# Norms by one power operation on GpSimd: a two-layer convolution, HGRN2 and retention block on one core

## The chip, the core and the metric

The kernel runs on one core of a Trainium2 chip. The metric is the device time of one execution in microseconds (us). An engine is named as in the profile: PE (TensorE, matrix products), PEld (its loading of weights), DVE (VectorE), ACT (ScalarE), POOL (GpSimd), SP (SyncE, which issues the transfers).

## What is computed

A block of two layers on 256 tokens of width 2048, in float32. In each layer the input is projected into ten parts; three mixers work on them (a causal convolution of 31 taps over 512 channels, a gated linear recurrence of 6 heads, a retention of 6 heads); their outputs go through `w_out`, and a feed-forward network of width 8192 follows. Behind both residual sums stands a layer norm over the width. Each mixer has a norm of its own too. All of them need one over the square root of a variance or a mean square:

```python
def layer_norm(x, g, b):                       # over 2048, and over 512 in the convolution
    mu = jnp.mean(xf, axis=-1, keepdims=True)
    var = jnp.mean(jnp.square(xf - mu), axis=-1, keepdims=True)
    return (xf - mu) * lax.rsqrt(var + LN_EPS) * g + b

# recurrence: over each head's 128 columns, no mean is subtracted
o = o * lax.rsqrt(jnp.mean(jnp.square(o), axis=-1, keepdims=True) + LN_EPS)
# retention: over each head's 128 columns
o = ((o - mu) * lax.rsqrt(var + LN_EPS)).reshape(b, t, D_RET) * gn_g + gn_b

for l in range(DEPTH):
    proj = jnp.einsum('btd,de->bte', x, w_in[l])
    ...
    h = jnp.einsum('bte,ed->btd', mix, w_out[l])
    x = layer_norm(DEEPNORM_ALPHA * x + h, ln1_g[l], ln1_b[l])
    f = jnp.square(jax.nn.relu(jnp.einsum('btd,df->btf', x, w_ff1[l])))
    h = jnp.einsum('btf,fd->btd', f, w_ff2[l])
    x = layer_norm(DEEPNORM_ALPHA * x + h, ln2_g[l], ln2_b[l])
```

## The kernel before

**Products.** Weights (440 MB with everything else) stream in by transfers of 1 MB on SP's queue into three `raw` buffers. Each half of a transfer is a unit: ACT rounds it (the high part, L288), and DVE subtracts to get the low part (L291), into one of six `wp` buffers; PE then multiplies three times (high by high, high by low, low by high). In `xstat` (products at L313) two token tiles of 128 take turns over eight units of 512 columns; in `wstat` (L363, L365) the features stand on the partitions. For the last column group ahead of a layer norm (`tail=6`) the first token tile ends six units ahead of the second, and behind it (`head=6`) the first token tile of the next phase runs six units ahead, so that each tile's norm lies beside the other tile's products. In those phases the low parts of units 1 and 3 are left to POOL (`POOL_LO`, also L291).

**A layer norm** (`Norm`, two token tiles each, four of them in the run) goes, for one tile: the last residual sum (L942 or L944) and its statistics (L869) on DVE, mean and variance (L879) on DVE, one over the square root on POOL (L422 to L430), meanwhile on DVE three operations `(y - mean) * g` (L887), then three `y * rstd + b` (L893) on DVE, and for the fourth chunk one scaling on ACT (L897); each chunk is transposed by PE (L399) and split into high and low parts by ACT (L388) and DVE (L390), which are the operand of the next products. In the last norm of the run there are four L887 and four L893, and eight transfers of the result instead of transpositions.

**A mixer's norm**: two heads by two token tiles give four runs of 128 columns in one tile of PSUM. `norm_stats` (L541, L543) takes mean and variance on DVE. POOL makes four inverse square roots per partition (L670 or L759, then L407 to L414 and, in retention, L761 to L763), ACT scales (L679 in `hgrn`, L770 in `ret`, L823 in `conv`), PE transposes (L399). There are six such norms in `hgrn` and six in `ret` over the two layers, and four in `conv`, whose inverse square root has the same form as a layer norm's.

**The order of the work** is a plan made when the kernel is built. Every operation is given to a list scheduler (`Plan`) with a cost in us, what it reads and what it writes. `run` sends each operation out in the order of its simulated start; 0.22 us lie between operations of different engines that depend on each other and 0.13 between those of one engine. Each engine then executes its queue strictly in that order. A cost in the plan thus decides where an operation stands in the queues, and not how long it takes. Large products are PE's own stream (`main`); the operations of a layer norm have priority (`FIRST`, `NOW`); of what can start within 0.12 us the scheduler takes the most urgent. The costs: `dve(n, ptr)` = 0.00104 n + 0.069 + 0.06 ptr, a weight split on POOL 2.35, one small POOL operation `POOLC` = 0.26, the twelve of a layer norm's inverse square root 2.6.

Of the kernel before, what the change touches and what calls it, by code (L numbers as in the profile page):

```python
# [202 lines left out]
def block_kernel(ctx: ExitStack, tc: tile.TileContext, a: dict, out: bass.AP):  # L203
# [30 lines left out]
    POOLC = 0.26  # L234

# [168 lines left out]
    def rsqrt(var, s, c0, n):  # L404
        """1/sqrt of var + EPS, [P, n], by Newton's iteration, to float32; columns c0.. of s are its own."""
        v, y, t = (s[:, c0 + i * n:c0 + (i + 1) * n] for i in range(3))
        G.tensor_scalar(out=v, in0=var, scalar1=EPS, scalar2=None, op0=ALU.add)  # L407
        G.tensor_scalar(out=y.bitcast(I32), in0=v.bitcast(I32), scalar1=-0.5, scalar2=float(0x5F3759DF),
                        op0=ALU.mult, op1=ALU.add)
        for _ in range(3):  # L410
            G.tensor_tensor(out=t, in0=y, in1=y, op=ALU.mult)  # L411
# [2 lines left out]
            G.tensor_tensor(out=y, in0=t, in1=y, op=ALU.mult)  # L414
        return y

    def rsqrt1(s, mean, var):
        """Columns 37, 48 of s: 1/sqrt(var + EPS) and -mean/sqrt(var + EPS), [P, 1], by Newton's iteration.
        The iterate is y times -2, 4, -8 in turn; v / 4, v / 16 make up for it."""
        v, v4, v16, y, t = (s[:, 52 + i:53 + i] for i in range(5))  # L420
        ts = G.tensor_scalar
        ts(out=v, in0=var, scalar1=EPS, scalar2=None, op0=ALU.add)  # L422
        ts(out=y.bitcast(I32), in0=v.bitcast(I32), scalar1=-0.5, scalar2=float(0x5F3759DF), op0=ALU.mult, op1=ALU.add)
        ts(out=v4, in0=v, scalar1=0.25, scalar2=None, op0=ALU.mult)
        ts(out=v16, in0=v, scalar1=0.0625, scalar2=None, op0=ALU.mult)
        for w in (v, v4, v16):
            ts(out=t, in0=y, scalar1=y, scalar2=w, op0=ALU.mult, op1=ALU.mult)  # L427
            ts(out=y, in0=t, scalar1=-3.0, scalar2=y, op0=ALU.add, op1=ALU.mult)  # L428
        ts(out=s[:, 37:38], in0=y, scalar1=-0.125, scalar2=None, op0=ALU.mult)  # L429
        ts(out=s[:, 48:49], in0=mean, scalar1=y, scalar2=0.125, op0=ALU.mult, op1=ALU.mult)  # L430
# [104 lines left out]
    def norm_stats(po, n, w):  # L535
        """Mean and variance (columns 24.. of the tile) of each of n runs of w columns."""
        s = sm.buf()

        def fn():
            for i in range(n):  # L540
                V.bn_stats(out=s.t[:, 6 * i:6 * i + 6], in_=po.t[:, i * w:(i + 1) * w])  # L541
            for i in range(n):
                V.bn_aggr(out=s.t[:, 24 + 2 * i:26 + 2 * i], in_=s.t[:, 6 * i:6 * i + 6])  # L543
# [49 lines left out]
    def hgrn(l, p, pair, gate, vt, mixT):
# [71 lines left out]
        s = norm_stats(po, 4, P)  # L665

        def rs():
            mv = s.t[:, 24:32].rearrange("p (n two) -> p n two", two=2)
# [1 line left out]
            G.tensor_tensor(out=q, in0=mv[:, :, 0], in1=mv[:, :, 0], op=ALU.mult)  # L670
# [49 lines left out]
    def ret(l, p, pair, gate, vt, mixT):  # L720
# [461 lines left out]
```

## Time and profile before

| | |
|---|---|
| median of three runs | 2399.02 us (2397.52 to 2400.28) |
| profiled execution, span | 2401.9 us |
| PE busy | 2343.3 us (98%) |
| DVE busy | 1505.0 us (63%) |
| ACT busy | 1052.9 us (44%) |
| POOL busy | 162.6 us (7%), 359 operations |
| read from memory | 432.74 MB, 181 GB/s over the span |

The profile is one execution; its span, 2401.9 us, is the only time it has of its own. A line of an operation gives the source line, the engine, the operation, its output and input tiles with their shapes, and how often it ran; in a timeline the first two numbers are the start and the length, and the brackets tell how long the engine had stood idle and what ended that. In a table of windows stand the stretch, its length, and the busy time of each engine; `PEclk` is the clock granted to PE, 1.00 at full speed. In the list of waits stand the total, the number and the longest one.

### The profile page before, as it was taken

How to read it: one execution, taken by the hardware profiler on the slowest of the kernel's cores; microseconds unless marked ns; L12 is line 12 of the kernel's file. 1: busy time of each engine (PE TensorE's matmuls, PEld its weight loads, DVE VectorE, ACT ScalarE, POOL GpSimd, SP SyncE). 2: the span in 40 equal slices, each digit the busy share in tenths (PEclk: the TensorE clock that was granted, in tenths of full speed). 3: DMA queues.
4: the chain of work that ended last, by engine and by line, in shares of the span. 5: the costliest groups of instructions: out<-in, count | busy, mean ns of one | idle time of the engine just before them, and what ended most of it. 6: DMA issues, size and time to landing. Idle time of an engine off the chain costs nothing.

```text
span 2401.9 us, 29886 instructions
## 1 busy us (share of the span) xinstructions
PE 2343.3 (98%) x12067; PEld 1986.8 (83%) x12067; DVE 1505.0 (63%) x2010; ACT 1052.9 (44%) x1334; POOL 162.6 (7%) x359
## 2 busy tenths in 40 slices
PE   9999999999999999999999999998999999999997
PEld 7888888788888888888778888887888888888886
DVE  6987565665465565565569975656655655655655
ACT  6435444354344344344344454443543443443441
POOL 0012021200000000000100031112000000000001
PEclk9999999999999999999999999999999999999999
DMA  8544556455555555556454445554555555555562
GB/s 287 181 158 144 181 176 202 158 184 186 195 181 192 193 190 188 195 182 217 160 169 161 162 149 169 191 202 152 190 193 193 180 190 193 191 193 193 178 228 103
DMA packets 67706, 439.91 MB, mean 183 GB/s; under 512 B 7664, under 2 KB 7920, under 8 KB 16624
## 3 DMA queue, kind: packets, MB, share of 16 engines
q1 hardware_dynamic: 67568, 438.01, 53.5%
q8 instruction: 94, 1.54, 0.2%
q14 instruction: 44, 0.36, 0.0%
HBM read 432.74 MB, written 2.10 MB: 181 GB/s over the span
## 4 chain that ended last, share of the span: by engine, by line
PE 88%; POOL 6%; issue 3%; DVE 2%; DMA 0%; ACT 0%; SPq 0%; DVEq 0%; POOLq 0%
PE mm L313 41%; PE mm L363 29%; PE mm L365 15%; PE aux L617 1%; PE aux L399 1%; DVE x_nat L893 1%; POOL sm L413 1%; POOL sm L411 1%; POOL sm L427 1%; POOL sm L412 1%; POOL sm L428 0%; DMA raw<-in_wv 0%; POOL sm L414 0%; DVE sm L541 0%; POOL sm L407 0%
## 5 line engine op out<-in xcount | busy, mean ns | idle before, releaser
L291 DVE TENSOR_TENSOR wp<-raw,wp 128x1024 fp32r<-128x1024 f32 (+1 forms) x796 | 970.8, 1220 | 626.8 <-ACT wp L288 624.7
L288 ACT CAST wp<-raw 128x1024 fp32r<-128x1024 f32 (+1 forms) x802 | 842.3, 1051 | 824.7 <-PE mm L313 567.7
L363 PE MATMUL mm<-act,wp 128*128 128x512 f32 x3328 | 1184.4, 400 | 0.0
L313 PE MATMUL mm<-wp,act 128*128 128x512 f32 x4608 | 1068.6, 392 | 3.5 <-ACT wp L288 2.5
L313 PEld LDWEIGHTS mm<-wp,act 128*128 128x128 f32 x4608 | 867.7, 189 | 184.5 <-ACT wp L288 3.5
L365 PE MATMUL mm<-act,wp 128*128 128x256 f32 x3328 | 934.9, 281 | 0.0
L363 PEld LDWEIGHTS mm<-act,wp 128*128 128x128 f32 x3328 | 627.2, 188 | 152.3
L365 PEld LDWEIGHTS mm<-act,wp 128*128 128x128 f32 x3328 | 629.8, 189 | 0.5
L372 ACT COPY r<-mm 128x256 f32<-128x256 f32 x208 | 77.9, 374 | 368.2 <-PE mm L365 368.0
L375 DVE TENSOR_TENSOR r<-mm,r 128x256 f32<-128x256 f32 x184 | 78.1, 425 | 152.5 <-ACT r L372 152.1
L422 POOL TENSOR_SCALAR sm<-sm 128x1 f32<-128x1 f32 x12 | 5.8, 486 | 1598.3 <-DVE sm L879 1594.7
L800 DVE SCALAR_TENSOR_TENSOR r<-u_t,cst,r 128x256 f32<-128x256 f32 x240 | 102.0, 479 | 0.0
L388 ACT CAST act<-r 128x512 fp32r<-128x512 f32 x82 | 51.1, 623 | 17.2 <-DVE r L1053 16.2
L390 DVE TENSOR_TENSOR act<-r,act 128x512 fp32r<-128x512 f32 x82 | 56.0, 683 | 3.9 <-ACT act L388 3.9
L893 DVE SCALAR_TENSOR_TENSOR x_nat<-x_nat,sm,r 128x512 f32<-128x512 f32 x26 | 30.5, 1231 | 22.4 <-POOL sm L429 22.4
L617 PEld LDWEIGHTS aux<-pair 128*128 128x128 f32 x336 | 42.4, 191 | 2.6
L1053 DVE SCALAR_TENSOR_TENSOR r<-r 128x512 f32<-128x512 f32 x60 | 41.6, 693 | 2.1
L399 PE MATMUL aux<-cst,x_nat 128*128 128x128 f32 x96 | 17.6, 335 | 25.2 <-DVE x_nat L893 16.4
L617 PE MATMUL aux<-pair 128*128 128x64 f32 x336 | 42.0, 267 | 0.0
L944 DVE TENSOR_TENSOR x_nat<-x_nat,mm 128x512 f32<-128x512 f32 x48 | 30.9, 681 | 12.6 <-PE mm L313 12.6
L399 PEld LDWEIGHTS aux<-cst,x_nat 128*128 128x128 f32 x96 | 13.4, 170 | 29.9 <-DVE x_nat L893 19.4
L670 POOL TENSOR_TENSOR sm<-sm 128x4 f32<-128x4 f32 x6 | 4.7, 790 | 424.1 <-DVE sm L543 424.1
(123 smaller groups left out, 661.3 us busy)
## 6 DMA issues: line engine op xcount, KB each, us to landing
raw<-in_w SPq DMA_DIRECT2D x248, 1024.0 KB, 4.8
raw<-in_wp SPq DMA_DIRECT2D x88, 1024.0 KB, 4.8
raw<-in_wo SPq DMA_DIRECT2D x32, 1024.0 KB, 4.8
raw<-in_wv SPq DMA_DIRECT2D x20, 1024.0 KB, 4.8
raw<-in_w1x SPq DMA_DIRECT2D x8, 1024.0 KB, 4.9
raw<-in_wv SPq DMA_DIRECT2D x6, 512.0 KB, 5.8
pair<-pair SPq DMA_DIRECT2D x24, 128.0 KB, 2.3
x_nat<-in_x SPq DMA_DIRECT2D x1, 2048.0 KB, 9.4
```

Source lines behind the costliest of these rows:

```text
L288: S.copy(out=u.w.t[:, 0, sl], in_=raw.t[:, rs])
L291: (G if pool_lo else V).tensor_tensor(out=u.w.t[:, 1, sl], in0=raw.t[:, rs], in1=u.w.t[:, 0, sl].bitcast(F32), op=ALU.subtract)
L313: nc.tensor.matmul(ps.t, lhsT=xT[k // 4].t[:, xs, k % 4, t * P:(t + 1) * P], rhs=w[:, ws, kb, :], start=(k == 0 and n == 0), stop=(k == KB ...
L363: nc.tensor.matmul(pv, lhsT=w[:, 0, kb, :], rhs=xt[:, :, k % 4, :], start=(k == 0), stop=False)
L365: nc.tensor.matmul(pv[:, 0, :], lhsT=w[:, 1, kb, :], rhs=xt[:, 0, k % 4, :], start=False, stop=(k == KB - 1))
L372: S.copy(out=low.t, in_=ps.t[:, T:])
L375: V.tensor_tensor(out=dst[2]()[:, b * T:(b + 1) * T], in0=ps.t[:, 0:T], in1=low.t, op=ALU.add)
L390: op("DVE", dve(n), lambda: V.tensor_tensor(out=x.t[:, 1, blks, cols], in0=bl(src(), nb), in1=x.t[:, 0, blks, cols].bitcast(F32), op=ALU.s ...
L399: nc.tensor.transpose(out=pt.t[:, i * P:(i + 1) * P], in_=src()[:, i * P:(i + 1) * P], identity=ident)
L617: nc.tensor.matmul(ps.t[:, b * 64:(b + 1) * 64], lhsT=Kt()[:, b * P:(b + 1) * P], rhs=rhs, start=True, stop=True)
L800: V.scalar_tensor_tensor(out=d, in0=src, scalar=cw[:, l, b, j:j + 1], in1=d, op0=ALU.mult, op1=ALU.add)
L893: op("DVE", dve(W, 1), lambda c=c: V.scalar_tensor_tensor(out=self.y(t, c), in0=self.y(t, c), scalar=rstd(), in1=self.gb[c][1].t, op0=ALU. ...
```

## The change

Newton's iteration (an estimate by integer arithmetic on the bits, then three steps) is taken out. A constant tile `mhalf` of -0.5, four columns, is written once, and one `tensor_tensor` with the operation `pow` on POOL raises variance plus epsilon to it. The sum with epsilon, and in the mixers the square of the mean (`square`) or the factor (`scaled`), move to DVE, right behind the statistics and in the same operation of the plan. -mean * rstd (L430 before) stays on POOL behind the power. The costs of the plan follow: `POW` = 1.5 for the power, 0.1 more for the statistics of a layer norm, 0.14 more for those of a mixer. Comments are removed as well.

```diff
-    POOLC = 0.26
+    POOLC, POW = 0.26, 1.5
...
-    def rsqrt(var, s, c0, n):
-        v, y, t = (s[:, c0 + i * n:c0 + (i + 1) * n] for i in range(3))
-        G.tensor_scalar(out=v, in0=var, scalar1=EPS, scalar2=None, op0=ALU.add)
-        G.tensor_scalar(out=y.bitcast(I32), in0=v.bitcast(I32), scalar1=-0.5, scalar2=float(0x5F3759DF),
-                        op0=ALU.mult, op1=ALU.add)
-        for _ in range(3):
-            G.tensor_tensor(out=t, in0=y, in1=y, op=ALU.mult)
-            G.tensor_tensor(out=t, in0=t, in1=v, op=ALU.mult)
-            G.tensor_scalar(out=t, in0=t, scalar1=-0.5, scalar2=1.5, op0=ALU.mult, op1=ALU.add)
-            G.tensor_tensor(out=y, in0=t, in1=y, op=ALU.mult)
+    def rsqrt(v, s, c0, n):
+        y = s[:, c0:c0 + n]
+        G.tensor_tensor(out=y, in0=v, in1=mhalf.t[:, 0:n], op=ALU.pow)
         return y
...
-    def rsqrt1(s, mean, var):
-        ... twelve tensor_scalar operations on [P, 1]
+    def rsqrt1(s, mean, v):
+        y = rsqrt(v, s, 37, 1)
+        G.tensor_scalar(out=s[:, 48:49], in0=mean, scalar1=y, scalar2=-1.0, op0=ALU.mult, op1=ALU.mult)
...
+    mhalf = keep("mhalf", [P, 4])
+    op("POOL", 0.2, lambda: G.memset(mhalf.t, -0.5), w=[mhalf])
...
-    def norm_stats(po, n, w):
+    def norm_stats(po, n, w, then, r=()):
...
+            then(s.t)
-        op("DVE", n * (dve(w) + 0.09), fn, r=[po], w=[s])
+        op("DVE", n * (dve(w) + 0.09) + 0.14, fn, r=[po, *r], w=[s])
...  hgrn
-        s = norm_stats(po, 4, P)
-        def rs():
-            mv = s.t[:, 24:32].rearrange("p (n two) -> p n two", two=2)
-            q = s.t[:, 32:36]
-            G.tensor_tensor(out=q, in0=mv[:, :, 0], in1=mv[:, :, 0], op=ALU.mult)
-            G.tensor_tensor(out=q, in0=q, in1=mv[:, :, 1], op=ALU.add)
-            rsqrt(q, s.t, 36, 4)
-        op("POOL", 16 * POOLC, rs, w=[s])
+        def square(s):
+            mv = s[:, 24:32].rearrange("p (n two) -> p n two", two=2)
+            q = s[:, 32:36]
+            V.tensor_tensor(out=q, in0=mv[:, :, 0], in1=mv[:, :, 0], op=ALU.mult)
+            V.scalar_tensor_tensor(out=q, in0=q, scalar=EPS, in1=mv[:, :, 1], op0=ALU.add, op1=ALU.add)
+        s = norm_stats(po, 4, P, square)
+        op("POOL", POW, lambda: rsqrt(s.t[:, 32:36], s.t, 40, 4), r=[mhalf], w=[s])
...  ret
+        def scaled(s):
+            ...
+            V.tensor_tensor(out=q, in0=mv[:, :, 1], in1=gq2, op=ALU.mult)
+            V.tensor_scalar(out=q, in0=q, scalar1=EPS, scalar2=None, op0=ALU.add)
-        op("POOL", 18 * POOLC, rs, r=[cst], w=[s])
+        op("POOL", POW + 3 * POOLC, rs, r=[cst, mhalf], w=[s])
...  conv
-            s = norm_stats(pn, 1, W)
+            s = norm_stats(pn, 1, W, lambda s: V.tensor_scalar(
+                out=s[:, 26:27], in0=s[:, 25:26], scalar1=EPS, scalar2=None, op0=ALU.add))
-            op("POOL", 2.6, rs, w=[s])
+            op("POOL", POW + POOLC, rs, r=[mhalf], w=[s])
...  Norm.norm
-            op("DVE", 0.1, lambda: V.bn_aggr(out=s.t[:, 24:26], in_=s.t[:, 0:24]), w=[s], **FIRST)
+            def aggr():
+                V.bn_aggr(out=s.t[:, 24:26], in_=s.t[:, 0:24])
+                V.tensor_scalar(out=s.t[:, 26:27], in0=s.t[:, 25:26], scalar1=EPS, scalar2=None, op0=ALU.add)
+            op("DVE", 0.2, aggr, w=[s], **FIRST)
-            op("POOL", 2.6, rs, r=[(s, "x")], w=[(s, "r")], **FIRST)
+            op("POOL", POW + POOLC, rs, r=[(s, "x"), mhalf], w=[(s, "r")], **FIRST)
```

More of the change, by code (lines that the diff above doesn't have):

```diff
@@ L402, in transpose4 @@
         return pt
-    def rsqrt(var, s, c0, n):
-        v, y, t = (s[:, c0 + i * n:c0 + (i + 1) * n] for i in range(3))
-        G.tensor_scalar(out=v, in0=var, scalar1=EPS, scalar2=None, op0=ALU.add)
-        G.tensor_scalar(out=y.bitcast(I32), in0=v.bitcast(I32), scalar1=-0.5, scalar2=float(0x5F3759DF),
-                        op0=ALU.mult, op1=ALU.add)
-        for _ in range(3):
-            G.tensor_tensor(out=t, in0=y, in1=y, op=ALU.mult)
-            G.tensor_tensor(out=t, in0=t, in1=v, op=ALU.mult)
-            G.tensor_scalar(out=t, in0=t, scalar1=-0.5, scalar2=1.5, op0=ALU.mult, op1=ALU.add)
-            G.tensor_tensor(out=y, in0=t, in1=y, op=ALU.mult)
-        return y
-    def rsqrt1(s, mean, var):
[L420 to L430, printed above, removed]
+    def rsqrt(v, s, c0, n):
+        y = s[:, c0:c0 + n]
+        G.tensor_tensor(out=y, in0=v, in1=mhalf.t[:, 0:n], op=ALU.pow)
+        return y
+    def rsqrt1(s, mean, v):
+        y = rsqrt(v, s, 37, 1)
+        G.tensor_scalar(out=s[:, 48:49], in0=mean, scalar1=y, scalar2=-1.0, op0=ALU.mult, op1=ALU.mult)
     NOW, FIRST = dict(slack=-50.0, floor=-100.0), dict(slack=-200.0, floor=-300.0)
+    mhalf = keep("mhalf", [P, 4])
+    op("POOL", 0.2, lambda: G.memset(mhalf.t, -0.5), w=[mhalf])
     def load_c():
@@ L750, in ret @@
                                   St.t[:, (2 * h + 1) * P:(2 * h + 2) * P]), [St, Sx], vt, 768 + 2 * p * P)
-        s = norm_stats(po, 4, P)
         gq = C["gq"][:, 4 * p:4 * p + 4]
         gq2 = C["gq2"][:, 4 * p:4 * p + 4]
+        def scaled(s):
+            mv = s[:, 24:32].rearrange("p (n two) -> p n two", two=2)
+            q = s[:, 32:36]
+            V.tensor_tensor(out=q, in0=mv[:, :, 1], in1=gq2, op=ALU.mult)
+            V.tensor_scalar(out=q, in0=q, scalar1=EPS, scalar2=None, op0=ALU.add)
+        s = norm_stats(po, 4, P, scaled, [cst])
         def rs():
             mv = s.t[:, 24:32].rearrange("p (n two) -> p n two", two=2)
-            q, nb = s.t[:, 32:36], s.t[:, 48:52]
-            G.tensor_tensor(out=q, in0=mv[:, :, 1], in1=gq2, op=ALU.mult)
-            y = rsqrt(q, s.t, 36, 4)
+            nb = s.t[:, 48:52]
+            y = rsqrt(s.t[:, 32:36], s.t, 40, 4)
             G.tensor_tensor(out=y, in0=y, in1=gq, op=ALU.mult)
@@ L815, in conv @@
             op("PE", 0.44, tr, r=accs + [cst], w=[pn])
-            s = norm_stats(pn, 1, W)
+            s = norm_stats(pn, 1, W, lambda s: V.tensor_scalar(
+                out=s[:, 26:27], in0=s[:, 25:26], scalar1=EPS, scalar2=None, op0=ALU.add))
             def rs(s=s):
-                rsqrt1(s.t, s.t[:, 24:25], s.t[:, 25:26])
-            op("POOL", 2.6, rs, w=[s])
+                rsqrt1(s.t, s.t[:, 24:25], s.t[:, 26:27])
+            op("POOL", POW + POOLC, rs, r=[mhalf], w=[s])
             on, sg, z = r2.buf(), r2.buf(), r2.buf()
@@ L878, in norm @@
             mean, rstd, nb = (lambda: s.t[:, 24:25]), (lambda: s.t[:, 37:38]), (lambda: s.t[:, 48:49])
-            op("DVE", 0.1, lambda: V.bn_aggr(out=s.t[:, 24:26], in_=s.t[:, 0:24]), w=[s], **FIRST)
+            def aggr():
+                V.bn_aggr(out=s.t[:, 24:26], in_=s.t[:, 0:24])
+                V.tensor_scalar(out=s.t[:, 26:27], in0=s.t[:, 25:26], scalar1=EPS, scalar2=None, op0=ALU.add)
+            op("DVE", 0.2, aggr, w=[s], **FIRST)
             def rs():
-                rsqrt1(s.t, mean(), s.t[:, 25:26])
-            op("POOL", 2.6, rs, r=[(s, "x")], w=[(s, "r")], **FIRST)
+                rsqrt1(s.t, mean(), s.t[:, 26:27])
+            op("POOL", POW + POOLC, rs, r=[(s, "x"), mhalf], w=[(s, "r")], **FIRST)
             direct = range(4) if self.last else [c for c in range(4) if c not in LAZY]
```

## The prediction

> **What bounds the kernel now.** I read the page's engine table first, then the windows around each norm, the chain, the waits, and the timelines of one layer norm, one mixer norm and the end.
>
> ```profile
> span 2401.9 us, 29886 instructions
> PE 2343.3 (98%) x12067; PEld 1986.8 (83%) x12067; DVE 1505.0 (63%) x2010; ACT 1052.9 (44%) x1334; POOL 162.6 (7%) x359
> ```
>
> The span is 2.9 us (0.12%) above the median of the three runs, 2399.0 us. I work out the change of the span and subtract it from the median. TensorE is busy for 98% of it; 58.6 us are not, and only those, and matmuls at a low clock, can be won. The windows show where they lie (columns: stretch, its length, then busy us of PE, PEld, DVE, ACT, POOL, the granted clock, DMA):
>
> ```profile
> 0.00:20.00 20.00, 15.31 (x47) 9.60 (x48) 10.71 (x13) 11.28 (x13) 0.39 (x5) 0.87 0.84 286
> 20.00:455.00 435.00, 427.56 (x2338) 366.48 (x2337) 311.79 (x540) 198.83 (x279) 51.33 (x126) 0.99 0.55 186
> 455.00:503.00 48.00, 39.30 (x175) 32.02 (x174) 31.84 (x37) 21.87 (x32) 16.49 (x26) 0.89 0.32 111
> 503.00:1182.00 679.00, 679.00 (x3423) 575.62 (x3422) 386.99 (x408) 293.06 (x337) 0.00 (x0) 1.00 0.57 194
> 1182.00:1230.00 48.00, 39.09 (x171) 31.79 (x170) 31.20 (x36) 21.71 (x31) 16.77 (x26) 0.89 0.32 107
> 1230.00:1650.00 420.00, 413.67 (x2278) 355.09 (x2277) 299.57 (x513) 191.31 (x275) 52.07 (x126) 1.00 0.52 176
> 1650.00:1700.00 50.00, 42.37 (x192) 34.39 (x192) 34.56 (x39) 23.94 (x35) 15.93 (x26) 0.93 0.37 126
> 2376.00:2401.90 25.90, 11.00 (x49) 8.78 (x47) 14.16 (x22) 0.00 (x0) 9.61 (x24) 0.78 0.21 81
> ```
>
> In the feed-forward stretch (503 to 1182) PE never stops and POOL does nothing. The three layer norms inside the run lose 8.7, 8.9 and 7.6 us (25.2), the two mixer stretches 7.4 and 6.3 (13.8), the last norm 14.9, the start 4.7. Everything but the start lies where POOL works on an inverse square root. PE's own waits say the same:
>
> ```profile
> PE aux L399 <- DVE x_nat L893: 16.4, 9, 2.2
> PE aux L399 <- ACT x_nat L897: 8.8, 3, 3.5
> PE aux L399 <- ACT r L679: 6.9, 4, 1.8
> PE aux L399 <- ACT r L770: 3.8, 6, 0.8
> PE aux L399 <- ACT r L823: 2.7, 2, 1.7
> PE mm L313 <- DVE wp L291: 1.0, 2, 0.8
> ```
>
> L399 is the transposition behind a norm. L893, L897, L679, L770 and L823 are the scalings that wait for POOL's result. One layer norm in the order of time (start, length, engine, what):
>
> ```profile
> 459.61 0.26 DVE L879 BATCH_NORM_AGGREGATE sm<-sm 128x2 f32<-128x24 f32 x1
> 459.91 2.08 DVE L887 SCALAR_TENSOR_TENSOR x_nat<-x_nat,sm,r 128x512 f32<-128x512 f32 x3
> 459.96 0.80 POOL L422 TENSOR_SCALAR sm<-sm 128x1 f32<-128x1 f32 x1 [84.14 <-DVE sm L879]
> ...
> 466.26 6.28 DVE L893 SCALAR_TENSOR_TENSOR x_nat<-x_nat,sm,r 128x512 f32<-128x512 f32 x3 [3.13 <-POOL sm L429]
> 466.42 5.57 POOL L291 TENSOR_TENSOR wp<-raw,wp 128x1024 fp32r<-128x1024 f32 x2
> ...
> 467.07 1.09 PE L399 MATMUL aux<-cst,x_nat 128*128 128x128 f32 x8 [2.21 <-DVE x_nat L893]
> ...
> 469.84 1.11 PE L399 MATMUL aux<-cst,x_nat 128*128 128x128 f32 x4 [1.68 <-DVE x_nat L893]
> ...
> 472.59 1.11 PE L399 MATMUL aux<-cst,x_nat 128*128 128x128 f32 x4 [1.64 <-DVE x_nat L893]
> ...
> 473.36 9.44 PE L313 MATMUL mm<-wp,act 128*128 128x512 f32 x36
> ...
> 478.40 0.25 DVE L879 BATCH_NORM_AGGREGATE sm<-sm 128x2 f32<-128x24 f32 x1
> ...
> 484.86 2.08 DVE L893 SCALAR_TENSOR_TENSOR x_nat<-x_nat,sm,r 128x512 f32<-128x512 f32 x3 [2.55 <-POOL sm L429]
> ...
> 485.96 1.97 PE L399 MATMUL aux<-cst,x_nat 128*128 128x128 f32 x8 [3.17 <-ACT x_nat L897]
> ```
>
> From the end of the statistics to the first L893 there are 6.4 us in the first token tile (459.87 to 466.26) and 6.2 in the second. PE comes to the transpositions and stands: 2.2 us for POOL, 1.7 and 1.6 because L893 is slow, 3.2 in the second tile. L893 is slow because POOL splits weights at that time: three of them take 6.28 us, against 2.08 in the second tile, at POOL's pace of 2.8 us an operation. After the pauses the clock is low as well: 36 matmuls take 9.44 us, against 8.2 at the pace of the steady part (quoted next, 87.05 / 384).
>
> ```profile
> 573.22 87.05 PE mm L313 x384
> ```
>
> The mixers (first head pair) and the end:
>
> ```profile
> 120.47 0.36 DVE L543 BATCH_NORM_AGGREGATE sm<-sm 128x2 f32<-128x6 f32 x4
> 120.92 1.08 POOL L670 TENSOR_TENSOR sm<-sm 128x4 f32<-128x4 f32 x1 [120.00 <-DVE sm L543]
> 129.53 1.14 ACT L679 ACTIVATE r<-aux,sm 128x128 f32<-128x128 f32 x4 [3.23 <-POOL sm L414]
> 129.95 1.25 PE L399 MATMUL aux<-cst,r 128*128 128x128 f32 x4 [1.85 <-ACT r L679]
> ```
>
> ```profile
> 2390.31 0.26 DVE L879 BATCH_NORM_AGGREGATE sm<-sm 128x2 f32<-128x24 f32 x1
> 2390.61 2.74 DVE L887 SCALAR_TENSOR_TENSOR x_nat<-x_nat,sm,r 128x512 f32<-128x512 f32 x4
> 2396.19 2.74 DVE L893 SCALAR_TENSOR_TENSOR x_nat<-x_nat,sm,r 128x512 f32<-128x512 f32 x4 [2.84 <-POOL sm L429]
> ```
>
> The planner gave 16 x 0.26 + 0.44 = 4.6 us to the mixer's chain; it took 8.7 (120.83 to 129.53). So the transposition stood in PE's queue about 4.1 us too early; 2.2 of that were absorbed by work between, and 1.85 became a pause. What costs the time is POOL being late against the plan, not POOL being slow as such.
>
> **The change part by part.** The operations on small tiles:
>
> ```profile
> L411 POOL TENSOR_TENSOR sm<-sm x36: 199/200/1455, 123.2 to 1569.0; 128x4 f32<-128x4 f32 x36
> L527 DVE TENSOR_SCALAR lbs<-lbs 128x6 f32<-128x6 f32 x1 | 0.2, 171 | 0.0
> ```
>
> (1) Removed: 12 to 18 POOL operations per norm, each 0.2 us when alone and up to 1.5 when a long VectorE operation runs beside it. (2) Added on VectorE: one operation per layer or convolution norm (12 norms), two per mixer norm (12): 36 at 0.17 us and a gap, some 7 us over the span. VectorE is busy for 63% and PE waited 1.0 us in all for its weights; this hides. On a norm's path they cost 0.2 or 0.4 us. Uncovered it would be 7 us. (3) One memset on POOL at the start: nothing waits for it before the first norm.
>
> (4) The power itself. No row shows one. Below, it is one POOL operation, 0.2 us. Above, it is as long as what it replaces, some 6 us; more is the rival below. The elements are no measure: a weight split of 1024 columns takes 2.8 us, so 1 or 4 columns are nothing, and what counts is a fixed price. The diff's planner puts 1.5. Its other weights lie close to rows (0.26 for a POOL operation whose row has 0.20 and a gap; 0.66 for an L887, of which three take 2.08), so I take 1.5, in the lower part of 0.2 to 6, and keep both ends.
>
> (5) What it does to VectorE meanwhile. Short POOL operations leave no mark: three L887 beside four of them take 2.08 us, as three L893 do alone. A long one does: L893 waits out POOL's weight split, 2.8 us each. A power of 1.5 us is nearer to the long ones, so I let it go between the first L887 and the second and hold the rest. The Trainium skill ("SBUF — State Buffer", the terms' shared port pair) says that a VectorE operation with two SBUF inputs and a GpSimd operation exclude each other for the whole instruction; by that rule, too, the power holds L887, and the trace agrees for the long operation (2.8 us), while for the short ones nothing is to be seen. By the rule the sum is the one below, by the short operations it is rival A's, 9 us less.
>
> So the first L893 of a tile starts after 0.25 (sum with epsilon) + 0.69 (one L887) + 1.5 + 2 x 0.69 + 0.05 = 3.9 us instead of 6.4 and 6.2: 2.5 and 2.3 us earlier. With no hold it starts when three L887 are done, after 2.4 us: 3.9 earlier.
>
> (6) The plan moves too. Its weight for the layer norm goes from 2.6 to 1.5 + 0.26. With two crossings of 0.22 that puts L893 2.2 us behind the statistics, when the three L887 end (2.1); before it was 3.0, and the planner filled the gap with a weight split of 1.1 us and let L893 go at 3.3. So L893, and the transposition in PE's queue, come about 1.0 us earlier in the plan. The first pauses of the other two norms:
>
> ```profile
> 1193.55 1.09 PE L399 MATMUL aux<-cst,x_nat 128*128 128x128 f32 x8 [2.13 <-DVE x_nat L893]
> ```
>
> ```profile
> 1662.51 1.09 PE L399 MATMUL aux<-cst,x_nat 128*128 128x128 f32 x8 [1.65 <-DVE x_nat L893]
> ```
>
> What PE sees is the difference: 1.5 us less pause in the first tile (of 2.2, 2.1 and 1.65: 4.5 in three norms), 1.3 in the second (of the 8.8 us at L897: 3.9). The pauses behind the slow L893 (two per norm; of the 16.4 us at L893 the 10.4 that are left) stay: POOL's weight splits follow the power at once and meet L893 as before. Sum for the three norms: 8.4 us of 25.2.
>
> (7) Mixers: the chain becomes 0.4 + 0.1 + some 0.7 (waiting for a VectorE operation) + 1.5 = 2.7 us against 0.14 + 1.5 + 0.44 = 2.1 in the plan: 0.6 late instead of 4.1. Retention has three more POOL operations in both, 0.8 late. Both are under the 2.2 us that were absorbed. Of PE's 6.9 + 3.8 + 2.7 = 13.4 us I take 12, and leave 1.4 for scalings that are late for other reasons. The power holds VectorE for 1.5 us in 16 such places, 24 us; its slack hides that, by the 1.0 us above.
>
> (8) Clock. Low clock cost 9.44 - 8.2 = 1.3 us on those 36 matmuls, and 1.97 instead of 1.1 for eight transpositions; with the few matmuls behind some 3 us per layer norm, about 9. Fewer pauses give back perhaps a third, 3, and 2 in the mixers (the granted clock is 0.99 over 435 us there): 5.
>
> (9) End: the last L893 starts 2390.57 + 0.25 + 0.69 + 1.5 + 3 x 0.69 = 2395.1 instead of 2396.2: 1.1 us, all of it on the path. With no hold, 2.6.
>
> Sum: 8.4 + 12 + 5 + 1.1 = 26.5 us. 2399.0 - 26.5 = 2372.5, **2372 us**.
>
> **Rivals.** (A) The power does not hold VectorE, or is well under 1 us. Then the first tiles' pauses go (6.0), the second tiles' shrink by up to 2.7 each (7.6), mixers 12, clock 7, end 2.6: 35.2, **2364**. For it: L887 beside short operations. Against: the 2.8 us.
>
> (B) The power is long, the rival on the other side. Per tile of a layer norm the pause changes by p - 2.9 us (3.9 - 1.5 + 1.0 against 6.3), six tiles; the mixers' gain of 12 holds until p - 0.9 exceeds the 2.2 us absorbed (p = 3.1), then 12 norms lose 1 us per us; the end changes by p - 2.6. At p = 3: +0.6 - 12 + 0.4 - 2 = -13, 2386. At 4: +6.6 - 2.6 + 1.4 = +5. It decides from p of about 3.7. At 6: 18.6 + 22 + 3.4 = +44, **2443**. For it: a power is no single step of an adder, and nothing here times one. Against: 12 to 18 POOL operations take only 6 to 9 us, most of that waiting.
>
> (C) The first power alone is as slow as all that it replaces, 6 us more, at 120 us in the run: a chain of 8.7 us against 2.1 planned, 6.6 late less 2.2, a pause of 4.4 instead of 0: **2377**. No row shows a slow first operation on POOL (the first L670 took 1.08 beside a VectorE split). The Trainium skill ("GPSIMD Engine Reference", Instruction dispatch) has such a price, about 6 us at the first call of freshly loaded code; whether the power is such code no run here shows.
>
> (D) The new order of all queues costs elsewhere what the norms give, for one: the weight split pushed behind L893 now makes the first products of the next phase wait. L893 would end at 470, the split at 471.2; PE gets there at about 473. It decides with 2 us more delay; if all three norms then lose 8 us, and the mixers half their gain: **2397**, no change.
>
> **How the numbers follow.** Forecast (power of 1 to 3 us, with hold) 0.52, A 0.22, C 0.06, D 0.06, B 0.14 (slower 0.12, 0.02 at no change). Less than 0.2% (4.8 us) is about what a measurement of this kernel cannot tell from no change. Faster 0.81, same 0.07, slower 0.12. The range goes from 2354 (A with the slow L893 gone too, half of 10.4 and more clock) to 2392 (a power of 3.3 us); outside are most of B and D and little below. The likeliest case alone: 2364 to 2386.
>
> **What would show it.** Step 4: the duration of the power in the groups on POOL. Step 5: three L887 that take 3.6 us, not 2.1. Step 6: aggregate to L893 3.9 us; PE's waits for L893 down from 16.4 to some 12, for L897 from 8.8 to 5. Step 7: the waits for L679, L770 and L823 nearly gone. Step 8: the clock in the norm windows above 0.89. Step 9: last L893 4.5 us behind the aggregate. It is wrong if the power is above 3 us, if PE waits for L291 in the new trace, or if the pauses come back under another name.

## The result and the profile after

The changed kernel takes 2340.88 us (median of four runs, 2339.74 to 2341.85), the kernel before 2399.43 in the same comparison: a ratio of 0.9754, interval 0.9742 to 0.9766. That is 58.5 us less, where 26.5 were forecast (2372), and below the range of 2354 to 2392. The profiled executions differ by 62.7 us (spans 2401.9 and 2339.2). A span lies 1.8 us below the time of its execution (2341.02 after), so the profiled execution of before lies about 4 us above its median; the tables below account for the 62.7.

First the page of the changed kernel: span, then busy time of each engine.

```profile
span 2339.2 us, 29616 instructions
PE 2320.4 (99%) x12067; PEld 1974.0 (84%) x12067; DVE 1504.0 (64%) x2046; ACT 1054.0 (45%) x1334; POOL 65.0 (3%) x66
```

PE has the same 12067 matmuls. Of the 62.7 us, 39.8 are idle time that is gone (58.6 before, 18.8 now), and 22.9 are *busy* time (2343.3 to 2320.4). The windows of the same stretches of both kernels say where; columns as in the prediction's windows. Before (start, mixers, layer norm, layer norm, mixers, layer norm, end):

```profile
0.00:85.52 85.52, 80.83 (x397) 65.78 (x398) 63.66 (x108) 48.63 (x61) 0.39 (x5) 0.96 0.76 267
85.52:379.15 293.63, 286.19 (x1654) 247.54 (x1653) 216.25 (x401) 131.53 (x201) 51.33 (x126) 0.99 0.49 163
379.15:573.22 194.07, 185.37 (x906) 155.66 (x905) 120.90 (x134) 85.50 (x106) 16.49 (x26) 0.97 0.54 182
...
1105.72:1282.37 176.65, 167.74 (x802) 140.33 (x802) 114.61 (x146) 77.61 (x96) 16.77 (x26) 0.97 0.54 181
1282.37:1575.16 292.79, 286.46 (x1653) 247.71 (x1653) 215.17 (x402) 134.81 (x209) 52.07 (x126) 0.99 0.48 164
1575.16:1767.41 192.25, 184.62 (x905) 154.95 (x905) 120.81 (x134) 85.37 (x106) 15.93 (x26) 0.98 0.54 184
...
2299.93:2401.90 101.97, 87.07 (x385) 71.73 (x383) 55.75 (x64) 29.35 (x29) 9.61 (x24) 0.94 0.45 159
```

After:

```profile
0.00:83.36 83.36, 79.48 (x397) 63.94 (x398) 63.37 (x108) 48.55 (x61) 0.43 (x6) 1.00 0.77 274
83.36:363.02 279.66, 279.64 (x1653) 245.68 (x1653) 217.97 (x415) 132.14 (x201) 16.55 (x19) 1.00 0.50 169
363.02:547.03 184.01, 182.41 (x905) 153.06 (x905) 118.90 (x135) 85.37 (x105) 9.38 (x6) 1.00 0.58 196
...
1079.53:1245.65 166.12, 164.61 (x803) 137.47 (x802) 113.02 (x148) 77.54 (x96) 9.45 (x6) 1.00 0.56 193
1245.65:1525.41 279.76, 279.76 (x1653) 245.93 (x1653) 218.12 (x416) 135.55 (x209) 16.15 (x19) 1.00 0.51 169
1525.41:1709.44 184.03, 182.46 (x905) 153.00 (x905) 118.88 (x135) 85.38 (x105) 9.37 (x6) 1.00 0.58 196
...
2241.94:2339.20 97.26, 87.07 (x385) 71.75 (x383) 55.78 (x66) 29.36 (x29) 3.70 (x4) 0.96 0.49 167
```

The mixers give 13.97 + 13.03 = 27.0 us, the three layer norms 10.06 + 10.53 + 8.22 = 28.8, the end 4.7, the start 2.2; the feed-forward stretches between take 532.5 us in both. The idle time of the mixers was 7.4 and 6.3 and is 0.02 and 0.00; that of the layer norms was 25.2 and is 4.7.

PE's waits now. L889 is the old L893; the waits for the old L897 and for the mixers' scalings are gone from the list:

```profile
PE aux L399 <- DVE x_nat L889: 3.5, 3, 1.2
...
PE mm L313 <- ACT act L388: 1.2, 3, 0.4
PE mm L313 <- DVE wp L291: 1.0, 2, 0.8
```

One layer norm in the order of time, first token tile (L872 is the aggregate, L873 the sum with epsilon, L883 the old L887, L407 the power):

```profile
443.46 0.27 DVE L872 BATCH_NORM_AGGREGATE sm<-sm 128x2 f32<-128x24 f32 x1
443.76 0.15 DVE L873 TENSOR_SCALAR sm<-sm 128x1 f32<-128x1 f32 x1
443.83 2.07 DVE L883 SCALAR_TENSOR_TENSOR x_nat<-x_nat,sm,r 128x512 f32<-128x512 f32 x3
444.06 0.95 POOL L407 TENSOR_TENSOR sm<-sm,mhalf 128x1 f32<-128x1 f32 x1 [87.55 <-DVE sm L873]
...
445.82 4.20 DVE L889 SCALAR_TENSOR_TENSOR x_nat<-x_nat,sm,r 128x512 f32<-128x512 f32 x3
445.91 2.90 POOL L291 TENSOR_TENSOR wp<-raw,wp 128x1024 fp32r<-128x1024 f32 x1
...
449.41 1.32 PE L399 MATMUL aux<-cst,x_nat 128*128 128x128 f32 x8 [1.19 <-DVE x_nat L889]
...
452.90 2.41 POOL L291 TENSOR_TENSOR wp<-raw,wp 128x1024 fp32r<-128x1024 f32 x1 [4.09 <-ACT wp L288]
```

Three L883 take 2.07 us beside the power: they are not held. L889 starts 2.09 us after the aggregate's end instead of 6.4. The first weight split on POOL still meets the second L889 (three take 4.20 instead of 2.07) and leaves one pause of 1.19 us. The second split used to start right behind the first: its high part, made by ACT (L288), was ready at 469.20, when the first split ended (469.23). Now it waits 4.09 us for that high part and runs at 452.90, when L889 is over. Numbers 1 and 2 below show that this comes from the new order of ACT's queue and not from POOL being free early.

The price of the power, by the groups on POOL:

```profile
L407 POOL TENSOR_TENSOR sm<-sm,mhalf 128x4 f32<-128x4 f32 x12 | 18.9, 1576 | 651.3 <-DVE sm L656 441.4 <-DVE sm L744 209.9
L407 POOL TENSOR_TENSOR sm<-sm,mhalf 128x1 f32<-128x1 f32 x12 | 11.5, 956 | 1601.2 <-DVE sm L873 1589.4 <-DVE sm L807 11.6
```

Alone it is shorter: 0.55 us on one column, 1.02 on four.

```profile
191.71 0.55 POOL L407 TENSOR_TENSOR sm<-sm,mhalf 128x1 f32<-128x1 f32 x1 [5.79 <-DVE sm L807]
...
240.85 1.02 POOL L407 TENSOR_TENSOR sm<-sm,mhalf 128x4 f32<-128x4 f32 x1 [46.10 <-DVE sm L656]
```

At the end of the run L889 follows the last aggregate by 2.76 us, not 5.62:

```profile
2330.49 0.26 DVE L872 BATCH_NORM_AGGREGATE sm<-sm 128x2 f32<-128x24 f32 x1
...
2333.51 2.73 DVE L889 SCALAR_TENSOR_TENSOR x_nat<-x_nat,sm,r 128x512 f32<-128x512 f32 x4
```

### The profile page after: what moved, and what is told of

The parts are those of the page before. It is cut to its first block, busy times and chain, and to the rows that moved or that the text cites. A ratio compares the mean times of both kernels' runs of the same rounds, so it can differ in the third digit from the quotient of the medians.

```text
span 2339.2 us, 29616 instructions
## 1 busy us (share of the span) xinstructions
PE 2320.4 (99%) x12067; PEld 1974.0 (84%) x12067; DVE 1504.0 (64%) x2046; ACT 1054.0 (45%) x1334; POOL 65.0 (3%) x66
## 4 chain that ended last, share of the span: by engine, by line
PE 98%; DVE 1%; DMA 0%; ACT 0%; issue 0%; SPq 0%; DVEq 0%
PE mm L313 44%; PE mm L363 33%; PE mm L365 17%; PE aux L604 2%; PE aux L399 1%; DVE x_nat L889 0%; DMA raw<-in_wv 0%; PE aux L550 0%; PE aux L552 0%; PE aux L588 0%; PE aux L548 0%; PE aux L717 0%; DVE x_nat L883 0%; ACT r L913 0%; DVE sm L861 0%
## 5 line engine op out<-in xcount | busy, mean ns | idle before, releaser
L291 DVE TENSOR_TENSOR wp<-raw,wp 128x1024 fp32r<-128x1024 f32 (+1 forms) x796 | 970.9, 1221 | 602.4 <-ACT wp L288 600.6
L288 ACT CAST wp<-raw 128x1024 fp32r<-128x1024 f32 (+1 forms) x802 | 842.4, 1052 | 819.0 <-PE mm L313 561.7
L407 POOL TENSOR_TENSOR sm<-sm,mhalf 128x4 f32<-128x4 f32 (+1 forms) x24 | 30.4, 1266 | 2252.5 <-DVE sm L873 1589.4
L388 ACT CAST act<-r 128x512 fp32r<-128x512 f32 x82 | 51.5, 628 | 21.7 <-DVE r L1049 16.2
L390 DVE TENSOR_TENSOR act<-r,act 128x512 fp32r<-128x512 f32 x82 | 57.9, 706 | 0.0
L938 DVE SCALAR_TENSOR_TENSOR x_nat<-x_nat,mm 128x512 f32<-128x512 f32 x32 | 20.6, 680 | 11.7 <-PE mm L313 11.7
L889 DVE SCALAR_TENSOR_TENSOR x_nat<-x_nat,sm,r 128x512 f32<-128x512 f32 x26 | 24.3, 989 | 0.0
L609 DVE COPY_PREDICATED r<-maskl,aux 128x256 f32<-128x256 uint8 x42 | 21.9, 521 | 0.0
L375 DVE TENSOR_TENSOR pair<-mm,r 128x256 f32<-128x256 f32 x24 | 10.2, 423 | 17.8 <-ACT r L372 17.8
```

The lines of the kernel that those rows point to most:

```text
L288: S.copy(out=u.w.t[:, 0, sl], in_=raw.t[:, rs])
L291: (G if pool_lo else V).tensor_tensor(out=u.w.t[:, 1, sl], in0=raw.t[:, rs], in1=u.w.t[:, 0, sl].bitcast(F32), op=ALU.subtract)
L375: V.tensor_tensor(out=dst[2]()[:, b * T:(b + 1) * T], in0=ps.t[:, 0:T], in1=low.t, op=ALU.add)
L388: op("ACT", act(n, ps=ps), lambda: S.copy(out=x.t[:, 0, blks, cols], in_=bl(src(), nb)), r=r, w=[(x, part)], **kw)
L390: op("DVE", dve(n), lambda: V.tensor_tensor(out=x.t[:, 1, blks, cols], in0=bl(src(), nb), in1=x.t[:, 0, blks, cols].bitcast(F32), op=ALU.s ...
```

## The experiments

The theory after the result (L, lateness): what costs time is how late POOL's result is against the plan, because a transposition that stands too early in PE's queue stops it and lowers its clock. The change gains twice, by a shorter chain and by plan costs that are true. The rivals: the new order of the queues is the gain, whatever the chain does; or POOL's work as such, or its hold on VectorE, is what cost the time. Each time is compared with the kernel before on the same chip, whose median was 2400.61 for the first four, 2401.49 for the next four and 2401.03 for the last four. Code is the changed kernel's unless told otherwise.

**1. The power with the plan of before.** The queues stand in the order of before, but for the 36 added operations.

```diff
-        op("POOL", POW, ...)                 # hgrn; ret: POW + 3 * POOLC; conv, Norm: POW + POOLC
+        op("POOL", 16 * POOLC, ...)          # ret: 18 * POOLC; conv, Norm: 2.6
```

> The power as in the changed kernel, but every cost in the plan as before (2.6 for a layer norm's inverse square root, 16 and 18 times 0.26 in the mixers, no extra for the sums with epsilon): the chain is short, the order of the queues is the old one. Theory L (PE loses what the chain is late against its place in the plan; the power ends that): the chain is now earlier than planned everywhere, 2341 to 2352 us, PE's and PEld's waits at the transpositions under 12 us. Rival R (the gain comes from the new order of the queues that the new weights make): at least half of it is given back, 2365 us or more.

2347.25, ratio 0.9776 (0.9761 to 0.9790). Most of the gain needs no new order; the order brings the last 5 to 6 us (5.3 by the ratios, 6.4 by the times). Its waits and a stretch of its first layer norm show which:

```profile
PE aux L399 <- DVE x_nat L889: 9.1, 6, 2.1
```

```profile
447.50 6.29 DVE L889 SCALAR_TENSOR_TENSOR x_nat<-x_nat,sm,r 128x512 f32<-128x512 f32 x3
447.60 5.64 POOL L291 TENSOR_TENSOR wp<-raw,wp 128x1024 fp32r<-128x1024 f32 x2
```

L889 starts 3.2 us behind the aggregate (444.28 to 447.50) instead of 2.1, because the old costs put a low part of VectorE ahead of it, and meets both weight splits: PE waits 9.1 us for it, against 3.5. POOL is free early here too, but in the old order ACT makes both high parts ahead of its L388 (two L288 from 448.40 to 450.39), and the second split follows at once.

**2. Newton's iteration with the new plan costs** (the kernel before, with the order of the changed one).

```diff
-        op("POOL", 16 * POOLC, rs, w=[s])    # and 18 * POOLC, 2.6, 2.6
+        op("POOL", POW, rs, w=[s])           # and POW + 3 * POOLC, POW + POOLC, POW + POOLC
```

> Newton's iteration as before, but with the costs of the changed kernel in the plan (1.5 in place of 4.2 and 2.6): the order of the queues is nearly the new one, the chain the old one. Theory L: a mixer's chain of 8.7 us stands against 2.1 planned instead of 4.6, so 2.5 us more per mixer norm (16 of them) and 1.0 per tile of a layer norm (6): about 46 us slower than before, 2430 to 2455. Rival R (the new order is the gain): faster than before, 2385 or less. Rival S (only the chain's length counts): 2399 within 5 us.

2432.15, ratio 1.0128 (1.0108 to 1.0148): the order alone loses 32 us. The rival that the order is the gain is out. PE's waits for the mixers' scalings are larger, 37.3 us against 13.4:

```profile
PE aux L399 <- ACT r L770: 14.9, 6, 2.7
PE aux L399 <- ACT r L679: 14.5, 6, 3.0
```

At the layer norms, where 1.0 us more per tile was expected, they fell, from 25.2 to 18.1. There the new order helps Newton's iteration as it helps the power, since it takes the second split away from L893:

```profile
489.67 2.41 POOL L291 TENSOR_TENSOR wp<-raw,wp 128x1024 fp32r<-128x1024 f32 x1 [4.74 <-ACT wp L288]
```

With the two kernels this makes a square: Newton 2399.4 in the old order and 2432.2 in the new, the power 2347.3 and 2340.9 (ratios 1, 1.0128, 0.9776, 0.9754). Both splits run back to back in the old order with either chain, and in the new order the second waits for ACT with either chain.

**3. Newton's iteration with costs as the trace measured them.**

```diff
-        op("POOL", 16 * POOLC, rs, w=[s])    # and 18 * POOLC, 2.6 (conv), 2.6 (Norm)
+        op("POOL", 8.2, rs, w=[s])           # and 8.2, 4.8, 5.8
```

> Newton's iteration as before, with the plan told what it took in the trace: 8.2 us in a mixer of heads, 4.8 in the convolution, 5.8 in a layer norm. Nothing on the chip is shorter. Theory L: the mixers' pauses go (PEld's waits for L679, L770 and L823, 21 us in the trace of before, and some low clock behind them), the layer norms keep most of theirs since PE runs out of other work there: 2365 to 2382 us. Rival S (the chain's length counts, not its place): 2399 within 5 us.

2372.59, ratio 0.9880 (0.9865 to 0.9895). No operation is taken out, and 28 of the 58.5 us are there. The mixers' waits are gone but for 2.0 us; 16.9 of the 25.2 us at the layer norms stay. That PE has no other work left there to fill a chain of 6 us is the likely reason, and was not tested:

```profile
PE aux L399 <- ACT x_nat L897: 9.3, 3, 3.3
PE aux L399 <- DVE x_nat L893: 7.6, 6, 1.6
PE aux L399 <- ACT r L823: 2.0, 2, 1.0
```

**4. The power in the layer norms alone**, with its costs; the mixers as before.

> The power, with its weight of 1.5, in the four layer norms alone; the mixers keep Newton and their old weights. Read from equal places in the two traces, the three inner layer norms gave 28.8 us of the 62.7 by which the spans differ, the last one 4.7, the mixers 27.0, the start 2.2. If these parts add up: 2399 - 33.5, so 2362 to 2370 us. If the gains of mixers and layer norms hang together (one order for all), it is over 2375 or under 2357.

2367.64, ratio 0.9859 (0.9843 to 0.9876), 33.0 us less than before. The layer norms and the end gave 28.8 + 4.7 = 33.5 in the windows: the gains of the two places add up.

**5. Eight small POOL operations ahead of each power**, on a scratch column.

```diff
+        for _ in range(8):
+            G.tensor_scalar(out=dum.t, in0=dum.t, scalar1=1.0, scalar2=None, op0=ALU.mult)
         G.tensor_tensor(out=y, in0=v, in1=mhalf.t[:, 0:n], op=ALU.pow)
```

> The changed kernel with eight small POOL operations (0.28 us from one to the next when alone, 2.3 us) ahead of every power; the order of all queues stays the changed kernel's. Theory L: a mixer's chain goes from 2.9 to 5.2 us against 2.1 planned, of which about 2.2 are absorbed: about 1 us on each of 16 mixer norms; a layer norm's L889 waits 1.5 to 2.3 us more, 8 to 12 us in six tiles; the end 2 to 4. Sum 2358 to 2380 us, most of the gain still there. By the prediction's formula for a long power (a break-even at 3.7 us, reached here with about 3.5): 2390 to 2402.

2350.59, ratio 0.9791 (0.9777 to 0.9804), less than expected. The experiment was badly built: the operations read nothing that VectorE writes, so POOL did them ahead of the statistics, in idle time, in most places. It shows that POOL's time as such costs little: 80.7 us of added operations cost some 9, and part of that is lateness all the same (PE has new waits of 5.0 us for ACT's scaling in the layer norms and 3.5 for the convolution's). Number 10 mends it.

**6. No weight splits on POOL.** `POOL_LO = ()` in place of `(1, 3)`.

> The changed kernel without weight splits on POOL (they go to VectorE, six in the run). In the changed kernel one of them still holds the second L889 of the first tile for 2.1 us, and PE pauses 1.2 us there, three times. If that collision is what is left: three L889 take 2.07 us, and the time is 2335 to 2339. If VectorE, which gets 1.2 us more work per split at its densest place, is late instead: 2341 to 2347, with new waits of PE for L291 or L390.

2348.57, ratio 0.9782 (0.9769 to 0.9795), just above the second forecast. Three L889 took 2.07 us and their pause was gone, but VectorE now came late with the weights, a loss above the gain:

```profile
PE mm L313 <- DVE wp L291: 9.2, 13, 1.9
```

**7. A second power, on 16 columns, ahead of the real one in each layer norm**, on scratch.

```diff
+                G.tensor_tensor(out=wide.t[:, 16:32], in0=wide.t[:, 0:16], in1=mhalf.t, op=ALU.pow)
                 rsqrt1(s.t, mean(), s.t[:, 26:27])
```

> The changed kernel with a second power, on 16 columns of a scratch tile, ahead of the real one in the layer norms alone. The shortest powers in the trace took 0.55 us on one column and 1.02 on four, 0.16 a column, so this one should take about 3 us. If a power holds VectorE's operations with two inputs while it runs (the prediction's step 5): three L883 take 4 us or more and the time is 2354 to 2368. If it does not: L883 stay at 2.07 us, L889 waits for the power alone, 2345 to 2356.

2341.58, ratio 0.9752 (0.9739 to 0.9766), the time of the changed kernel and below both forecasts. It too ran ahead or in idle time, so it did not lengthen the chain. But three of the eight fell on L890 (here L889's line), as this one:

```profile
461.61 3.42 POOL L878 TENSOR_TENSOR wide<-wide,mhalf 128x16 f32<-128x16 f32 x1
...
462.18 2.07 DVE L890 SCALAR_TENSOR_TENSOR x_nat<-x_nat,sm,r 128x512 f32<-128x512 f32 x3
```

This power of 3.42 us held none of them.

**8. The sum with epsilon back on POOL**, with the plan unchanged.

```diff
-                V.tensor_scalar(out=s.t[:, 26:27], in0=s.t[:, 25:26], scalar1=EPS, ...)   # and in the mixers
+        G.tensor_scalar(out=e, in0=v, scalar1=EPS, scalar2=None, op0=ALU.add)             # in rsqrt
```

> One part of the change undone: the sum with epsilon is POOL's again (one operation ahead of each power), and VectorE's 18 rows fewer; the plan is the same. Theory L: the chain is 0.3 to 0.7 us longer in POOL and 0.15 to 0.2 shorter on VectorE, which the slack takes: 2340 to 2345 us. If moving that sum is a part of the gain of its own: 2348 or more.

2345.23, ratio 0.9768 (0.9755 to 0.9782): between the two forecasts. The move to VectorE is worth some 3 to 4 us: 3.4 by the ratios, whose intervals overlap, and 3.65 against number 7, run beside it with the time of the changed kernel. The prediction had priced it only as 0.2 or 0.4 us on a norm's path, without a gain.

**9. The wide power in the chain**: it reads what VectorE wrote just before.

```diff
+                G.tensor_tensor(out=wide.t, in0=s.t[:, 26:27].broadcast_to([P, 16]), in1=mhalf.t, op=ALU.pow)
                 rsqrt1(s.t, mean(), s.t[:, 26:27])
```

> As the wide power before, but it now reads the variance of the tile (on 16 columns), so that it can't run ahead of the statistics: in each tile of the layer norms 3.4 us of power stand between the statistics and the real power, beside three L883 with two inputs each. No hold (VectorE works on while a power runs): L883 x3 stay at 2.07 us, L889 starts 4.4 to 4.8 us behind the statistics instead of 2.1, and the time is 2350 to 2358. Hold (prediction's step 5): L883 x3 take 4.5 us or more, L889 starts after 6 us, 2360 to 2370.

```profile
443.15 2.07 DVE L884 SCALAR_TENSOR_TENSOR x_nat<-x_nat,sm,r 128x512 f32<-128x512 f32 x3
443.31 3.36 POOL L878 TENSOR_TENSOR wide<-sm,mhalf 128x16 f32<-128x16 f32 x1 [87.37 <-DVE sm L873]
...
447.22 4.20 DVE L890 SCALAR_TENSOR_TENSOR x_nat<-x_nat,sm,r 128x512 f32<-128x512 f32 x3 [2.01 <-POOL sm L407]
```

Three L884 take 2.07 us beside a power of 3.36: the hold of step 5 does not exist. The time was 2360.00, ratio 0.9828 (0.9812 to 0.9845), above the 2350 to 2358 of no hold and at the lower end of the hold's range; it is the rows that decide, and all eight tiles show L884 at this pace. L890 starts 4.2 us behind the statistics instead of 2.1, and that lateness cost 19 us (PE waits 7.8 for L890 and 6.5 for L894).

**10. Eight small operations in the chain of every norm**, now reading `v`.

```diff
+            G.tensor_scalar(out=dum.t, in0=v[:, 0:1], scalar1=1.0, scalar2=None, op0=ALU.mult)   # 8 times
```

> As the eight small POOL operations before, but they now read the variance, so that they stand in the chain of every norm: 2.3 us when alone, about 3.4 at the 0.42 us each that they took. The order of the queues is the changed kernel's. Theory L: between this order with the power's chain (2341) and with Newton's (2432) the time goes with the chain; a mixer's chain then is 6.2 us of 2.9 to 8.7, so about half way: 2375 to 2400 us. By the prediction's formula, with its break-even at a power of 3.7 us and this one equal to 4.5 to 5: 2408 or more.

```profile
119.45 5.04 POOL L408 TENSOR_SCALAR dum<-sm 128x1 f32<-128x1 f32 x8 [118.50 <-DVE sm L659]
...
125.52 1.14 ACT L667 ACTIVATE r<-aux,sm 128x128 f32<-128x128 f32 x4 [3.52 <-POOL sm L409]
```

2413.52, ratio 1.0053 (1.0038 to 1.0068): slower than before. Theory L's 2375 to 2400 missed; the prediction's formula (2408 or more) was nearer. The chain of the mixer is 6.55 us (the statistics end at 118.97, the scaling starts at 125.52), shorter than Newton's 8.7. But the plan says 2.1, so it is 4.45 late, and Newton was 4.1 late against a plan of 4.6. PE's waits for the mixers' scalings are 28.3 us, against 13.4 before; at the layer norms they are 15.8, against 25.2. That is lateness without length, and POOL is busy for less time than before (134.4 us against 162.6), which settles it against POOL's work as such.

**11 and 12. Other units for POOL's splits**: `POOL_LO = (3, 5)` and `(3,)`.

> The changed kernel with units 3 and 5 instead of 1 and 3 left to POOL: as many splits on VectorE as before, but none on POOL while L889 runs. If the collision of L889 with POOL's first split is what PE's last 3.5 us of pauses at L399 come from: L889 x3 take 2.07 us, 2336 to 2340. If unit 5's split on POOL comes too late for PE instead: 2340 to 2345, with PE waiting at L313 for POOL.

> The changed kernel with unit 3 alone left to POOL: one split per phase more on VectorE (1.2 us), none on POOL beside L889. VectorE is busy 10 of 10 us behind the first tile's norm in the changed kernel, and without any split on POOL it cost 8 us: 2341 to 2346. If VectorE's load there is no matter with one split more: 2336 to 2340.

2352.45, ratio 0.9797 (0.9783 to 0.9812), above both of its forecasts, and 2344.34, ratio 0.9765 (0.9750 to 0.9780), inside the first of its own. In both L889 is free, and PE waits for VectorE's low parts instead (8.5 us in number 12). In number 11:

```profile
PE mm L313 <- DVE wp L291: 12.5, 5, 3.8
```

```profile
452.99 5.16 POOL L291 TENSOR_TENSOR wp<-raw,wp 128x1024 fp32r<-128x1024 f32 x2 [6.38 <-ACT wp L288]
453.15 2.80 DVE L390 TENSOR_TENSOR act<-r,act 128x512 fp32r<-128x512 f32 x1
```

An L390, 0.68 us when alone, takes 2.80 beside the splits. Units 1 and 3 remain the best choice of the four tried, and no version was clearly faster than the changed kernel.

## Why the prediction was wrong

The sign and the mechanism were right: POOL late against the plan. Number 3 and number 10 show it from both sides. The sizes were not:

| step | forecast | measured |
|---|---|---|
| (5), (6) pauses at the three layer norms | 8.4 | 20.5 |
| (7) pauses in the mixers | 12 | 13.75 |
| (8) busy time of PE | 5 | 22.9: layer norms 8.25, mixers 13.25, start 1.35 |
| (9) end | 1.1 | 4.7 |
| idle time at the start | 0 | 0.8 |

**Step 5 failed: the power does not hold VectorE.** I let it stop VectorE for 1.5 us and weighed it with the long POOL operations; three L883 took 2.07 us beside it, and number 9 shows the same for 3.36 us. Without the hold, rival A's working gave 6.0 + 7.6 for the pauses of the two tiles; both went completely (6.0 + 8.8). Rival A had this step right, and its 2364 was still 23 us too high, for the reason under step 8. The Trainium skill ("SBUF — State Buffer", Terms) says that the pair of SBUF ports that VectorE and GpSimd share is held for the full instruction. For a weight split the runs agree (2.80 us for an L390 in number 11); for the power, which reads SBUF and meets a VectorE operation with two SBUF inputs, they do not, at either width.

**Step 6 failed in its last sentence.** The 10.4 us behind the slow L893 were to stay because the splits follow the power at once. The first does (445.91), the second waits 4.09 us for ACT (452.90). So 10.4 became 3.5. The cause is the new plan: in ACT's queue one L288 now stands ahead of the first L388, where two stood. The power in the old order keeps the collision (number 1: three L889 in 6.29 us), and Newton's iteration in the new order loses it (number 2). 6.0 + 8.8 + 6.9 = 21.7, less about 1.2 of small waits for L388, is the 20.5. I had asked what the new costs do to L893 and to the transposition, and not what else they reorder.

**Step 8 is the largest miss, 18 us.** I took PE's busy time for work. The transpositions behind the mixers show that it was not; before, then after, with the mean in ns behind the busy us:

```profile
L399 PE MATMUL aux<-cst,r 128*128 128x128 f32 x80 | 19.4, 308 | 13.8 <-ACT r L679 6.9 <-ACT r L770 3.8 <-ACT r L823 2.7
```

```profile
L399 PE MATMUL aux<-cst,r 128*128 128x128 f32 x80 | 12.3, 273 | 0.0
```

The same 80 transpositions were busy for 7.1 us more. They follow the scaling piece by piece, and a block of which each part waits for the next piece counts as busy. The waits of the weight loads, in the trace of before, tell it better than those of PE:

```profile
PEld aux L399 <- ACT r L770: 9.5, 24, 1.2
PEld aux L399 <- ACT r L679: 8.6, 5, 2.2
...
PEld aux L399 <- ACT r L823: 3.3, 2, 2.0
```

They sum to 21.4 us where PE's are 13.4; L770 was waited for 24 times and not 6. The clock is the smaller part in the mixers. In the trace of before it was 0.50 in one stretch of each mixer phase and behind the pauses of each layer norm; the first of both kinds:

```profile
130.76:134.16 3.40, 3.40 (x12) 2.92 (x12) 3.20 (x7) 1.12 (x2) 0.00 (x0) 0.50 0.13 53
468.68:475.48 6.80, 4.00 (x13) 3.21 (x14) 6.73 (x5) 4.00 (x9) 3.31 (x2) 0.50 0.57 172
```

The mixers' other one is as long, at 1393.7 us. PE was busy throughout both, at half the clock: an estimated 1.7 us lost in each, 3.4 of the mixers' 13.25. That leaves some 9.9 for waits inside PE's busy time, 7.1 of them in the transpositions' own row: a term that step 8 did not have. In the layer norms the clock was 0.50 for 27.3 us, in 20.5 of which PE was busy, so it cost at most 10.3 us there, enough for the 8.25; how much of that was waits was not separated. I had put it at about 9 and let a third come back; beside the one pause of 1.2 us that remains the clock stays at 1.00 in every 5 us slice from 442 to 467 us, and so nearly all of it did.

**Step 9.** The hold fell here too: aggregate to L889 takes 2.76 us, not 4.5, which gives 2.86 of the 4.7. The other 1.84 come from the tile before: its L893 no longer keeps the last residual sum waiting, which before started at 2388.87, 1.9 us after the last products.

**What held.** Step 2: VectorE's 36 operations are hidden (busy 1504.0 against 1505.0). Step 4: 1.5 us for the power, measured 0.96 and 1.58 in the mean; but that number was the planner's, and the reason given for it, a fixed price on which the columns do not tell, fell (0.55, 1.02 and 3.33 us on 1, 4 and 16 columns). Rival B's working for a long POOL chain: number 10, with 8 x 0.456 us ahead of powers of 0.58 and 1.04, stands for 4.2 us in the layer norms and 4.7 in the mixers of heads, for which it gives some +17 us, and lost 12.5; a turning point near 3.7 fits that. **What fell.** Rival C: the first power took 1.87 us, beside an L291 that had started before it, and the second 1.94. The price of a first call that the Trainium skill names ("GPSIMD Engine Reference", Instruction dispatch) is not to be seen. Rival D: PE waits 1.0 us for VectorE's L291, as before, and the new order gains 5 to 6 us. Three sums of the prediction do not come out as written, and the forecast does not rest on them: B's mixers at 4 us are -12 + 10.8 = -1.2 and not -2.6 (+7 in all, not +5); D's 2397 would be 2387 with 8 us lost at the three norms together, or 2403 with 8 at each; and the cases add up to 0.80 faster and 0.08 the same, not 0.81 and 0.07.

The 2.2 us at the start, where the change puts only a memset, come with a granted clock of 1.00 instead of 0.96 in the one execution of each kernel: before it was 0.50 for 6.8 us from 14.7 us on. Kernels with the change show this too (number 12 for 6.8 us from 15.4 us, numbers 7 and 11 for 3.4), so it belongs to the execution and not to the change.

## What to carry to other kernels

Where a list scheduler lays out strict queues, compare each cost in the plan with the duration in the trace first: making the costs true gave half of this gain without touching an operation, and a chain made shorter while its cost in the plan is made shorter still can lose. Price a late operand by the waits of the weight loads and by the busy time around it, not by the matmul engine's idle time alone. A changed cost moves every queue, also of engines that the change does not touch: here the place of one ACT operation decided whether POOL's second split met VectorE's scaling. Look through the whole new order for what it moves together or apart.

## What the runs showed of the hardware

A power on POOL costs 0.55 us on one column, 1.02 on four and 3.33 to 3.82 on sixteen, 0.16 to 0.19 us more per column, against 0.20 us for a small addition or product. It held none of VectorE's operations (three L883 in 2.07 us beside it). Some powers took longer beside VectorE's work: one column took 0.95 us beside an L883 that had started before it, four took 1.87 beside an L291 that ended 0.98 us into it. Others did not: one column took 0.56 us beside an L291 that started after it (192.73 us), and sixteen took 3.34 to 3.36 beside an L884 that had started before (number 9). A weight split of 1024 columns does hold VectorE's L889 and L390 (one L390 took 2.80 us). What sets the split apart from the power was not tested. In the kernel before, the granted clock was 0.50 for 6.8 us from 468.7 us on, where PE paused for 2.2, 1.7 and 1.6 us within 8 us, and for 3.4 us behind a single pause of 1.85 us (130.8 us). In the changed kernel it stayed at 1.00 behind a pause of 1.2 us.
